# Attention of a hybrid diffusion step: order of the rounds written out, scores of two heads in row halves, final norm on token partitions

## The chip, the cores and the metric

One core of a Trainium2 chip runs the whole program; its other cores are idle. The metric is the time of one execution in microseconds (us), the median of several. Five engines work side by side, each through its own queue in order: TensorE (PE; its weight loads have a row of their own, PEld), VectorE (DVE), ScalarE (ACT), GpSimd (POOL) and SyncE (SP), which here only issues transfers. A transfer that SP issues stands in SP's queue until its buffer is free, and all that is behind it stands too.

## The reference, cut to what matters

```python
x = x_prompt                                    # 128 tokens; then the same for 256 latent tokens
for l in range(2):
    sm, cm, gm, sf, cf, gf = adaln(cond, w_ada[l], b_ada[l])      # silu(cond) @ w_ada + b_ada
    h = rmsnorm(x, norm_mix_g[l]) * (1 + cm) + sm
    if l == 0:                                  # attention, 16 heads of 64
        q, k, v = qkv_proj(h, w_qkv[0])
        mix = merge_heads(attend(q, k, v)) @ w_attn_out[0]
    else:
        mix = chunk_gmlp(h, ...)
    x = x + gm * mix
    h = rmsnorm(x, norm_ffn_g[l]) * (1 + cf) + sf
    x = x + gf * conv_ffn(h, ...)               # width 2816, depthwise conv of width 3
y = rmsnorm(x, norm_final_g)
# attend, context: softmax(q k^T / 8) v over the 128 context keys
# attend, latent (grid of 4 x 64): softmax over [4 x 16 window: q k^T / 8 + rpb | 128 cached keys: q k^T / 8]
```

All data is float32. Outputs are y for both groups and the context keys and values.

## The kernel before, in words

The 384 tokens (128 context, 256 latent) lie on the free axis: `x[k]`, k = 0 to 7, holds 128 features by 384 tokens. Every weight block of 128 x 1024 (a unit of eight 128 x 128 pieces) is loaded by `load` (line 88): SP issues the transfer into a staging tile `st` (pool `stg`, three buffers), ACT rounds it to `hi` (line 96), DVE makes the rest `lo` (line 97). A product is three matmuls, hi x hi, hi x lo, lo x hi (`mac`, lines 103 to 105); PE does 24 of them for one unit.

Attention works on pairs of heads, t = 0 to 7. `keys(t)` makes the 128 features of a pair's keys (24 matmuls), copies them to `kT` (line 439) beside the cached keys, sends the context part out from POOL's queue (`out_skT`, line 440), and builds for each head a tile `ks` with the rounded keys on 64 partitions and their rest on the other 64. `queries(t)` builds `qd` (the rounded queries twice, lines 456 and 457) and `ql`. So a score block of one head (`score`, lines 464 and 465) is a contraction over all 128 partitions, for two latent row blocks (b = 0, 1; 384 keys each) and, with b = 0, the context rows (128 keys). `bias(t)` loads six runs of 64 numbers for each of 64 partitions and each of two rows and two heads (line 473), reversed in DVE's read and added to a mask (line 479). `scores` adds the bias over 256 columns with a running maximum (line 502), takes the maximum of the rest (506, 507, 511), exponentiates on ACT with the sum (486) and normalizes on DVE (487, 488). `turned` transposes a head's probabilities on PE (lines 523 to 528) and copies them to `pT` on ACT (524, 529). `values(t)` multiplies by the values, the two heads in the two column halves of the array (line 538), and splits the result to `ohi`, `olo`. `Ada` computes the modulation of the rest of the layer between the rounds: three blocks of `w_ada` per round, in the array's four column strips (line 190).

The Tile framework's scheduler decides in which order the instructions of a round stand on each engine, from its own model of when data is ready; the loop at the end of `attention` only gives the program order from which it starts. It mixes the splits of later weights, the exponentials and the queries of the next pair freely on ACT, and decides where on SP the loads stand. `kT` and the `ks` tiles have two buffers. The scores of a head use the two banks of `ps_sc` one after another.

After the last pair come the eight output units (`w_o`, from line 560 on, the first three without their last piece until the last pair's values are there), each followed by `residual` (line 366): gate and add on DVE (line 368), the square for the next norm (269, 271), and `early` (336, 337), which prepares the first units of the feed-forward part, for which `norm_first` (line 340) multiplies before the norm is known. The sums of squares are made on PE (line 280) at the place where the program has them.

At the end `rms` makes the inverse norm on token partitions, spreads it over all partitions with three matmuls (line 294), DVE multiplies each `x[k]` with it (line 742), and eight transfers of 192 KB leave from SP's and ACT's queues (line 743).

## Time and profile before

| | us |
|---|---|
| median of 3 runs (1028.15 to 1030.63) | 1030.49 |
| the profiled execution | 1030.51 |
| its span, first to last instruction | 1028.7 |
| outside the span | 1.8 |
| PE busy | 1001.3 (97%) |
| VectorE busy | 796.0 (77%) |
| ScalarE busy | 496.2 (48%) |

The busy shares are means over stages that differ: normalization and values up to 63 us, the rounds of attention and its output units up to 245 us, two feed-forward parts of 280 us each with the gating layer between them, and the final norm. An engine's idle time counts only where it ends last, so a stage is read by its windows, its waits and its timeline. PE's granted clock has a row of its own: 1.00 is 2.4 GHz, 0.50 is 1.2 GHz.

### The profile page before, as it was taken

What the parts mean: (1) busy time and instruction counts of PE and PEld (TensorE: products, weight loads), DVE (VectorE), ACT (ScalarE), POOL (GpSimd) and SP (SyncE); (2) the same over time, 40 slices, a digit from 0 to 9 for tenths busy, and PEclk for the clock granted to TensorE, in tenths of its full rate; (3) what the DMA queues carried; (4) which work ended last, traced back from release to release, by engine and by line L of the source; (5) the groups of instructions that cost most, each with busy time, mean ns of one, the idle gap of its engine ahead of it and who ended that gap; (6) DMA issues with size and microseconds to landing.
All of it is one profiled execution on the core that took longest, in us unless ns stands there. A gap on an engine that the chain in (4) does not pass through costs nothing.

```text
span 1028.7 us, 16012 instructions
## 1 busy us (share of the span) xinstructions
PE 1001.3 (97%) x5964; PEld 953.1 (93%) x5964; DVE 796.0 (77%) x1697; ACT 496.2 (48%) x862; POOL 14.1 (1%) x29
## 2 busy tenths in 40 slices
PE   7999897999999999999999999999999999999996
PEld 5787786899999999999998889999999999999995
DVE  3557777657998888899989989888598777777553
ACT  3357666656754555433345334433385444443330
POOL 1000000000000000000000000000000000000000
PEclk8999898999999999999999999999999999999998
DMA  7867766623355545476637756666325443335521
GB/s 282 308 196 204 204 192 219 217 76 141 108 185 166 165 156 159 135 237 216 217 123 248 245 167 191 183 204 194 106 83 164 143 124 123 124 113 174 163 63 62
DMA packets 64717, 174.32 MB, mean 169 GB/s; under 512 B 18800, under 2 KB 24064, under 8 KB 64640
## 3 DMA queue, kind: packets, MB, share of 16 engines
q1 hardware_dynamic: 63632, 171.46, 52.9%
q8 instruction: 47, 0.77, 0.3%
q0 software_dynamic: 432, 1.06, 0.3%
q10 hardware_dynamic: 576, 0.79, 0.2%
q14 instruction: 30, 0.25, 0.1%
HBM read 170.66 MB, written 2.62 MB: 168 GB/s over the span
## 4 chain that ended last, share of the span: by engine, by line
PE 88%; DMA 4%; DVE 3%; issue 2%; ACT 2%; POOL 0%; SPq 0%; POOLq 0%; DVEq 0%; ACTq 0%
PE bank L103 28%; PE bank L104 27%; PE bank L105 27%; DMA st<-in_w_qk 1%; PE bank L704 1%; PE bank L145 1%; DMA st<-in_w_o 1%; DMA btr<-in_rpb 1%; PE bank L190 1%; PE bank L538 1%; DMA out_skT<-kT 1%; PE bank L280 1%; PE bank L294 0%; ACT hi L96 0%; DMA cond<-in_cond 0%
## 5 line engine op out<-in xcount | busy, mean ns | idle before, releaser
L96 ACT CAST hi<-st 128x1024 fp32r<-128x1024 f32 (+1 forms) x216 | 222.6, 1033 | 325.8 <-PE bank L104 261.6
L104 PE MATMUL bank<-hlo,hi 128*128 128x384 f32 (+1 forms) x960 | 325.7, 339 | 0.0
L105 PE MATMUL bank<-hhi,lo 128*128 128x384 f32 (+1 forms) x960 | 325.6, 339 | 0.0
L103 PE MATMUL bank<-hhi,hi 128*128 128x384 f32 (+1 forms) x960 | 325.1, 339 | 0.0
L97 DVE TENSOR_TENSOR lo<-st,hi 128x1024 fp32r<-128x1024 f32 (+1 forms) x216 | 259.5, 1202 | 84.7 <-ACT hi L96 84.3
L103 PEld LDWEIGHTS bank<-hhi,hi 128*128 128x128 f32 x960 | 181.7, 189 | 0.9 <-issue 0.8
L105 PEld LDWEIGHTS bank<-hhi,lo 128*128 128x128 f32 x960 | 181.7, 189 | 0.0
L104 PEld LDWEIGHTS bank<-hlo,hi 128*128 128x128 f32 x960 | 181.0, 189 | 0.1
L248 DVE CUSTOM_DVE_ANT_0 junk<-adw,cs 128x1024 bf16<-128x1024 f32 x112 | 136.6, 1220 | 1.0
L105 PE MATMUL bank<-ahi,lo 128*128 128x384 f32 x352 | 118.9, 338 | 0.0
L104 PE MATMUL bank<-alo,hi 128*128 128x384 f32 x352 | 118.9, 338 | 0.0
L103 PE MATMUL bank<-ahi,hi 128*128 128x384 f32 x352 | 118.7, 338 | 0.0
L104 PEld LDWEIGHTS bank<-alo,hi 128*128 128x128 f32 x352 | 66.1, 188 | 0.0
L105 PEld LDWEIGHTS bank<-ahi,lo 128*128 128x128 f32 x352 | 66.1, 188 | 0.0
L103 PEld LDWEIGHTS bank<-ahi,hi 128*128 128x128 f32 x352 | 66.1, 188 | 0.0
L103 PE MATMUL bank<-hi,hhi 128*128 128x512 f32 x144 | 57.7, 404 | 1.8 <-ACT hhi L322 1.8
L105 PE MATMUL bank<-hi,hlo 128*128 128x512 f32 x144 | 57.5, 399 | 0.0
L104 PE MATMUL bank<-lo,hhi 128*128 128x512 f32 x144 | 57.4, 398 | 0.0
L368 DVE SCALAR_TENSOR_TENSOR x<-bank,mod,x 128x128 f32<-128x128 f32 x64 | 23.9, 413 | 38.8 <-PE bank L105 38.8
L103 PE MATMUL bank<-mhi,hi 128*128 128x384 f32 x128 | 43.3, 339 | 0.0
L105 PE MATMUL bank<-mhi,lo 128*128 128x384 f32 x128 | 43.2, 337 | 0.0
L104 PE MATMUL bank<-mlo,hi 128*128 128x384 f32 x128 | 43.1, 337 | 0.0
(150 smaller groups left out, 1262.5 us busy)
## 6 DMA issues: line engine op xcount, KB each, us to landing
st<-in_w_up SPq DMA_DIRECT2D x88, 512.0 KB, 3.6
adw<-in_w_adaT SPq DMA_DIRECT2D x56, 512.0 KB, 3.6
adw<-in_w_ada SPq DMA_DIRECT2D x40, 512.0 KB, 6.1
st<-in_w_down SPq DMA_DIRECT2D x32, 512.0 KB, 3.7
st<-in_w_qk SPq DMA_DIRECT2D x16, 512.0 KB, 7.1
st<-in_w_gu SPq DMA_DIRECT2D x16, 512.0 KB, 4.2
st<-in_w_gv SPq DMA_DIRECT2D x16, 512.0 KB, 4.5
st<-in_w_gout SPq DMA_DIRECT2D x16, 512.0 KB, 4.5
```

The lines of the kernel that those rows point to most:

```text
L96: nc.scalar.copy(hi[:, :n], st[:, :n])
L97: nc.vector.tensor_tensor(lo[:, :n], st[:, :n], hi[:, :n].bitcast(F32), ALU.subtract)
L103: nc.tensor.matmul(out, a[0], b[0], start=start, stop=False)
L104: nc.tensor.matmul(out, a[0], b[1], start=False, stop=False)
L105: nc.tensor.matmul(out, a[1], b[0], start=False, stop=stop)
L145: nc.tensor.matmul(pa[32 * j:32 * j + 32, 0:P], cond_s[:, 4 * hf + kk, :], w[hf][:, kk, P * q:P * q + P], start=(kk == 0), stop=(kk == 3), ...
L190: nc.tensor.matmul(self.pa[32 * j:32 * j + 32, 0:256], cond_s[:, k, :], t[:, 256 * j:256 * j + 256], start=(k == 0), stop=(k == KD - 1), t ...
L248: tc.keep_in_program_order(nc.vector.tensor_tensor_reduce(self.junk, t, self.cs[c], 1.0, 0.0, ALU.mult, ALU.add, m[:, c:c + 1]))
L280: mm = nc.tensor.matmul(ss[:, 2 * b:2 * b + 2], src[:, b * P:(b + 1) * P], ones[:, 0:2], start=(i == 0 and b == 0), stop=(i == 1 and b == 2))
L368: nc.vector.scalar_tensor_tensor(x[m][:, a:b], ps[:, a:b], mod(l, gate, m, c), x[m][:, a:b], ALU.mult, ALU.add)
L538: nc.tensor.matmul(pv[64 * hh:64 * hh + 64, cols], vv[:, P * t + 64 * hh:P * t + 64 * hh + 64], pT[hh][:, o:o + n], start=start, stop=stop ...
L704: nc.tensor.matmul(pm[:, b * P:b * P + P], vn[g // 4][:, b, (g % 4) * P:(g % 4) * P + P], ws[:, g % 2, :], start=True, stop=True)
```

## The change: what it does

1. The attention stage from the first weight of the keys to the last piece of output unit 3 stands inside `tc.manual_schedule` for PE, ACT, DVE and SP: on these engines the program's order is the order of issue. POOL keeps its own.
2. Loads are apart from splits: `fetch` issues the next unit's transfer as soon as a staging tile has been split, `ready` splits the unit that came first. The order is keys 0, queries 0, keys 1, queries 1, ..., then the output units.
3. Both heads are scored together (`scores(b, ...)`): one tile of rounded keys and one of their rest (`khi`, `klo`), the same for queries (with the scale's sign turned). A head's contraction is over its own 64 partitions, three matmuls for each block, and the two heads alternate, into two banks. `qd` and `ks` are gone, and with them the zeroed halves.
4. The sign of the scores is turned, so the maximum becomes a minimum over all 384 columns in one DVE instruction with the bias (zeros stand between its parts, since the columns now lie as 128 latent, 128 cached, 128 latent), and `exp` takes scale -1. The reciprocals of a block are one instruction.
5. The bias of a pair comes in two transfers of 64 x 2 runs of 219 numbers (876 bytes); the six overlapping pieces are picked in DVE's read. `kT` and `btr` have one buffer.
6. The tail of attention is written out: where the last pair's transposes, values 6 and 7 and output units 0 to 3 stand.
7. At the end the eight `x[k]` are transposed to token partitions on PE while the norm is computed; three DVE and three ACT instructions multiply with the inverse norm of each token, and six transfers of 256 KB leave. The output `y` is token-major, so the host no longer transposes.

```diff
-    def sums(pin=False):
+    def sums(pin=False, between=None):
         ss = bank(ps_tb)
         for i, src in enumerate((sq["acc"], sq["last"])):
+            if i and between is not None:
+                between()
...
+        KPARTS = ((V[:, 1], 0), (cv, 256), (V[:, 2], 512))
+        def weights():
+            for t in range(NPAIR):
+                yield w_qk[1, t]
+                yield w_qk[0, t]
+            yield from (w_o[m] for m in range(KD))
+        coming = weights()
+        staged, units = [], []
+        def fetch():
+            src = next(coming, None)
+            if src is None:
+                return
+            st = stg.tile([P, 1024], F32, name="st", tag="st")
+            nc.sync.dma_start(st.rearrange("p (a b) -> p a b", b=P), src)
+            staged.append(st)
+        def ready():
+            st = staged.pop(0)
+            hi = whp.tile([P, 1024], F32R, name="hi", tag="hi")
+            lo = wlp.tile([P, 1024], F32R, name="lo", tag="lo")
+            split(hi, lo, st)
+            fetch()
+            units.append(tuple(p.rearrange("p (a b) -> p a b", b=P) for p in (hi, lo)))
...
+        def cache(t):
+            kT = wkp.tile([P, 512], F32, name="kT", tag="kT", bufs=1)
+            nc.sync.dma_start(kT[:, 256:384], ckT_in[:, t, :])
+            return kT
+        def keys(t, kT, p):
+            nc.scalar.copy(kT[:, 0:256], p[:, 0:256])
+            nc.scalar.copy(kT[:, 384:512], p[:, 256:384])
             nc.gpsimd.dma_start(skT_out[:, t, :], kT[:, 0:NPR])
-            ks = [wkp.tile([P, 512], F32R, name="ks", tag=f"ks{hh}", bufs=2) for hh in range(2)]
+            k = [wkp.tile([P, 512], F32R, name=n, tag=n) for n in ("khi", "klo")]
+            split(*k, kT)
+            return k
+        def queries(p):
+            q = [wkp.tile([P, NT], F32R, name=n, tag=n) for n in ("qhi", "qlo")]
+            s = -HD ** -0.5
+            nc.scalar.activation(q[0], p[:, :NT], AF.Copy, scale=s)
+            nc.vector.scalar_tensor_tensor(q[1], p[:, :NT], s, q[0].bitcast(F32), ALU.mult, ALU.subtract)
+            return q
...
+        def scores(b, q, k, sc):
+            for cols, qs, ks in ((slice(0, NT), NPR + b * P, slice(NPR, 512)),
+                                 (slice(NT, 512), 0, slice(0, NPR)))[:2 - b]:
+                for i, (qp, kp) in enumerate(((0, 0), (0, 1), (1, 0))):
+                    for hh in range(2):
+                        nc.tensor.matmul(sc[hh][:, cols], q[qp][HS[hh], qs:qs + P], k[kp][HS[hh], ks],
+                                         start=i == 0, stop=i == 2)
...
+        def exps(b, sc, pr, pc):
+                nc.vector.tensor_tensor_reduce(
+                    sc[hh][:, :NT], sc[hh][:, :NT],
+                    bt[:, hh, 2 - 2 * b:5 - 2 * b].rearrange("p g c -> p (g c)"),
+                    1.0, 3e38, ALU.add, ALU.min, st[:, 0, hh:hh + 1])
...
+        order = tc.manual_schedule(engines={mybir.EngineType.PE, mybir.EngineType.Activation,
+                                            mybir.EngineType.DVE, mybir.EngineType.SP})
+        order.__enter__()
+        for _ in range(3):
+            fetch()
+        kT, btr = cache(0), bias_load(0)
+        nc.sync.dma_start(cv, cv_in)
+        ada.load(3)
+        ready()
+        p = products()
+        ready()
+        K = keys(0, kT, p)
+        p = products()
+        ready()
+        bias(btr)
+        Q = queries(p)
         old = None
-        pT = None
         for t in range(NPAIR):
-            new = [scores(t, 0, qT, kT, bt)]
+            last = t == NPAIR - 1
+            pr = [wkp.tile([P, 2, NT], F32, name="pr", tag="pr", bufs=4) for _ in range(2)]
+            pc = [wkp.tile([P, NPR], F32, name="pc", tag="pc", bufs=4) for _ in range(2)]
+            sc = [bank(ps_sc) for _ in range(2)]
+            scores(0, Q, K, sc)
+            if not last:
+                kT, btr = cache(t + 1), bias_load(t + 1)
+            e = exps(0, sc, pr, pc)
             if old is not None:
-                pT = [turned(0, old)]
-            if t < NPAIR - 1:
-                kT2 = keys(t + 1)
-                bt2 = bias(t + 1)
+                two = turn(*old[0])
+            normalized(*e)
             if old is not None:
-                pT.append(turned(1, old))
-            new.append(scores(t, 1, qT, kT, bt))
-            if t < NPAIR - 1:
-                qT, kT, bt = queries(t + 1), kT2, bt2
+                pT = [turned(0, two)]
+            if not last:
+                p = products()
+            ready()
+            sc = [bank(ps_mm if last else ps_sc) for _ in range(2)]
+            scores(1, Q, K, sc)
+            if last:
+                ada.run(3)
+            else:
+                K = keys(t + 1, kT, p)
+            e = exps(1, sc, pr, pc)
             if old is not None:
-                values(t - 1, pT)
-            old = new
-            ada.load(3)
-            ada.run(3)
+                pT.append(turned(1, turn(*old[1])))
+            normalized(*e)
+            if not last:
+                p = products()
+                ready()
+                bias(btr)
+                Q = queries(p)
+                if old is not None:
+                    values(t - 1, pT)
+                ada.run(3)
+                ada.load(3)
+                old = [(pr[hh], pc[hh]) for hh in range(2)]
...
+        output(0, range(6), ps_mm)
+        ready()
+        values(6, pT, ps_sc)
+        output(1, range(6), ps_sc)
+        ready()
+        pT = [turned(0, turn(pr[0], pc[0]))]
+        output(0, (6,))
+        output(1, (6,))
+        pT.append(turned(1, turn(pr[1], pc[1])))
+        output(2, range(7), ps_mm)
+        ready()
+        values(7, pT)
+        output(3, range(7), ps_sc)
         ada.flush()
-        head = []
-        for m in range(KD):
-            w = load(w_o[m])
-            po = bank(ps_mm if m != 2 else ps_sc)
-            n = KD - 1 if m < 3 else KD
-            for k in range(n):
-                mac(po[:, :NT], wsel(w, k, allm), (ohi[k], olo[k]), k == 0, k == KD - 1)
-            if m < 3:
-                head.append((w, po))
-            else:
-                residual(0, GM, m, po, (0, SF, CF))
-            if m == 0:
-                pT = [turned(0, old)]
+        for m in range(4):
+            output(m, (7,))
+            residual(0, GM, m, out[m][1], (0, SF, CF))
+            if m == 1:
+                ready()
+        order.__exit__(None, None, None)
...
-    R = rms()
-    for k in range(KD):
-        nc.vector.tensor_tensor(x[k], x[k], R[:, :NT], ALU.mult)
-        (nc.sync, nc.scalar)[k % 2].dma_start(yT_out[:, k, :], x[k])
+    with tc.tile_pool(name="fin", bufs=1) as pool:
+        turned = [[bank(q) for q in two] for two in ((ps_ta, ps_ad), (ps_sc, ps_sc), (ps_mm, ps_mm))]
+        def turn(ks):
+            for k in ks:
+                for b in range(3):
+                    o = (k % 4) * P
+                    tc.keep_in_program_order(nc.tensor.transpose(
+                        turned[b][k // 4][:, o:o + P], x[k][:, b * P:(b + 1) * P], ident))
+        r = inverse(sums(True, lambda: turn(range(3))))
+        turn(range(3, KD))
+        for b in range(3):
+            for half in range(2):
+                y = pool.tile([P, 512], F32, name=f"y{b}{half}")
+                if half:
+                    nc.scalar.activation(y, turned[b][half], AF.Copy, scale=r[:, b:b + 1])
+                else:
+                    nc.vector.tensor_scalar(y, turned[b][half], r[:, b:b + 1], None, ALU.mult)
+                (nc.sync, nc.scalar)[half].dma_start(y_out[b, :, 512 * half:512 * half + 512], y)
```

On ACT, in round t = 5, from the last exponentials of the pair to its predecessor's outputs (`pr`, `pc` probabilities, `hi` a unit's rounded half, `qd` or `qhi` the next pair's queries). Before:

```order
L96 CAST hi_2263<-st_2262 128x1024
L486 ACTIVATE pr_1852,st_1854<-bank_1855,st_1854 128x384
L96 CAST hi_2303<-st_2302 128x1024
L486 ACTIVATE pc_1853,st_1854<-bank_1855,st_1854 128x128
L486 ACTIVATE pr_1852,st_1854<-bank_1870,st_1854 128x384
L456 ACTIVATE qd_1910<-bank_1885 64x384
L457 ACTIVATE qd_1910<-bank_1885 64x384
L96 CAST hi_2354<-st_2353 128x1024
```

Now:

```order
L534 ACTIVATE pr_1700,st_1795<-bank_1780,st_1795 128x384
L534 ACTIVATE pr_1701,st_1795<-bank_1781,st_1795 128x384
L556 COPY pT_1809<-bank_1800 128x512
L557 COPY pT_1809<-bank_1801 128x384
L108 CAST hi_1840<-st_1597 128x1024
L482 ACTIVATE qhi_1848<-bank_1815 128x384
L108 CAST ohi4_181<-bank_1852 128x384
```

Three splits of output units stood among the exponentials and ahead of the queries; now one split stands there, behind the exponentials and the transposed copies, of a unit that was fetched three splits earlier.

On DVE, in the same half of the round (`lo` a unit's rest, `bt` the bias, `qlo` the queries' rest, `olo` the outputs' rest). Now:

```order
L541 TENSOR_SCALAR pr_1700<-pr_1700,st_1795 128x384
L541 TENSOR_SCALAR pr_1701<-pr_1701,st_1795 128x384
L109 TENSOR_TENSOR lo_1841<-st_1597,hi_1840 128x1024
L507 TENSOR_TENSOR bt_718<-mask_161,btr_1720 128x3x128 x2
L483 SCALAR_TENSOR_TENSOR qlo_1849<-bank_1815,qhi_1848 128x384
L109 TENSOR_TENSOR olo4_189<-bank_1852,ohi4_181 128x384
```

The queries' rest, on which PE's next score block waits, is the last but one of a chain that begins with the exponentials.

On SP, from the load of pair 6's cached keys to that of pair 7's. Before:

```order
L434 DMA kT_1792<-in_ckT 128x128
L93 DMA st_1794<-in_w_qk 128x1024
L473 DMA btr_1833<-in_rpb 64x6x64 x2
L176 DMA adw_1737<-in_w_ada 128x1024
L176 DMA adw_1739<-in_w_ada 128x1024
L473 DMA btr_1833<-in_rpb 64x6x64 x2
L93 DMA st_1879<-in_w_qk 128x1024
L176 DMA adw_1929<-in_w_ada 128x1024
L93 DMA st_1995<-in_w_qk 128x1024
L434 DMA kT_1993<-in_ckT 128x128
```

Now:

```order
L468 DMA kT_1718<-in_ckT 128x128
L497 DMA btr_1720<-in_rpb 64x2x219 x2
L448 DMA st_1778<-in_w_o 128x1024
L448 DMA st_1844<-in_w_o 128x1024
L176 DMA adw_1882<-in_w_ada 128x1024
L176 DMA adw_1884<-in_w_ada 128x1024
L176 DMA adw_1886<-in_w_ada 128x1024
L468 DMA kT_1906<-in_ckT 128x128
```

The keys and the bias are now asked for first in a round, the bias in two transfers for four, and the two units that follow are already output units, three splits ahead.

## Rows read from the trace of the kernel before

**Rows 1.** The page: the granted clock in 40 slices of 25.7 us, and the chain of work that ended last, as shares of the span by engine.

```profile
PEclk8999898999999999999999999999999999999998
...
PE 88%; DMA 4%; DVE 3%; issue 2%; ACT 2%; POOL 0%; SPq 0%; POOLq 0%; DVEq 0%; ACTq 0%
```

**Rows 2.** The windows of three stages (rounds of attention and their outputs, first feed-forward part, final norm): length, busy time and count of each engine, granted clock, share of the DMA engines, GB/s.

```profile
56.00:250.00 194.00, 183.93 (x1210) 161.47 (x1210) 131.29 (x385) 123.56 (x273) 5.79 (x10) 0.96 0.60 186
...
250.00:530.00 280.00, 280.00 (x1603) 279.82 (x1602) 251.47 (x513) 135.70 (x215) 0.85 (x1) 1.00 0.55 171
...
1016.00:1028.70 12.70, 2.68 (x15) 2.24 (x14) 4.90 (x14) 1.14 (x2) 0.85 (x1) 0.61 0.35 124
```

**Rows 3.** What PE waited for between 63 and 250 us: total, times, longest.

```profile
PE bank L464 <- ACT qd L457: 6.9, 4, 4.7
PE bank L464 <- ACT pc L486: 1.8, 1, 1.8
PE bank L206 <- ACT ada_sb L195: 0.8, 1, 0.8
```

**Rows 4.** The windows of the two stretches at the lower clock in the rounds (columns as in rows 2).

```profile
121.10:127.92 6.82, 6.07 (x25) 4.86 (x26) 5.27 (x19) 4.32 (x11) 0.00 (x0) 0.50 0.80 236
172.30:179.12 6.82, 4.69 (x23) 2.98 (x27) 6.64 (x17) 4.99 (x13) 0.00 (x0) 0.50 0.59 215
```

**Rows 5.** The timeline around the longest gap, 168 to 176 us: start, length, engine, line, and in brackets the idle time before it and its releaser.

```profile
170.01 1.04 ACT L96 CAST hi<-st 128x1024 fp32r<-128x1024 f32 x1 [4.95 <-DMA st<-in_w_o]
...
173.86 0.48 ACT L457 ACTIVATE qd<-bank 64x384 fp32r<-64x384 f32 x1
...
174.40 1.01 PE L464 MATMUL bank<-ks,qd 128*128 128x384 f32 x2 [4.66 <-ACT qd L457]
```

**Rows 6.** The timeline of PE in a round without a wait, 135 to 147 us: end of a product, values, modulation, first score block, transposes, second score block.

```profile
135.36 0.34 PE L105 MATMUL bank<-hhi,lo 128*128 128x384 f32 x1
...
135.89 0.34 PE L105 MATMUL bank<-hhi,lo 128*128 128x384 f32 x1
136.16 1.08 PE L538 MATMUL bank<-pT,V 128*64 128x256 f32 x8
...
137.83 1.50 PE L190 MATMUL bank<-adw,cond_s 128*32 128x256 f32 x24
139.26 0.45 PE L464 MATMUL bank<-ks,qd 128*128 128x384 f32 x1
...
139.72 0.22 PE L464 MATMUL bank<-ks,qd 128*128 128x128 f32 x1
139.78 0.27 PE L465 MATMUL bank<-ks,ql 128*128 128x128 f32 x1
139.89 0.39 PE L464 MATMUL bank<-ks,qd 128*128 128x384 f32 x1
...
140.30 0.60 PE L523 MATMUL bank<-ident,pr 128*128 128x128 f32 x4
...
145.95 0.42 PE L464 MATMUL bank<-ks,qd 128*128 128x384 f32 x1
...
146.95 0.34 PE L103 MATMUL bank<-hhi,hi 128*128 128x384 f32 x1
```

**Rows 7.** Groups of instructions, shapes kept apart: count, busy us, mean ns of one, idle before.

```profile
L97 DVE TENSOR_TENSOR lo<-st,hi 128x1024 fp32r<-128x1024 f32 x200 | 244.3, 1222 | 82.5 <-ACT hi L96 82.2
L96 ACT CAST hi<-st 128x1024 fp32r<-128x1024 f32 x200 | 209.2, 1048 | 294.9 <-PE bank L104 241.0 <-PE bank L105 20.4 <-issue 11.4
...
L486 ACT ACTIVATE pr<-bank,st 128x384 f32<-128x384 f32 x32 | 18.4, 578 | 9.8 <-DVE st L507 9.6
...
L502 DVE CUSTOM_DVE_ANT_0 bank<-bank,bt 128x256 f32<-128x256 f32 x32 | 13.3, 440 | 1.1 <-PE bank L465 0.7
...
L445 DVE TENSOR_TENSOR ks<-kT,ks 64x512 fp32r<-64x512 f32 x16 | 11.0, 686 | 5.5 <-ACT ks L444 5.1
...
L524 ACT COPY pT<-bank 128x512 f32<-128x512 f32 x16 | 9.4, 586 | 9.9 <-PE bank L523 9.8
...
L479 DVE TENSOR_TENSOR bt<-btr,mask 128x768 f32<-128x768 f32 x8 | 7.7, 958 | 4.3 <-issue 2.6 <-DMA btr<-in_rpb 1.7
```

**Rows 8.** What SP's queue waited for between 60 and 215 us, and transfers between 73 and 197 us: KB each, median us from issue to landing.

```profile
SPq L434 <- DMA out_skT<-kT: 39.4, 5, 9.9
...
btr<-in_rpb SPq DMA_DIRECT2D x24, 96.0 KB, 7.1
...
out_skT<-kT POOLq DMA_DIRECT2D x7, 64.0 KB, 6.0
```

**Rows 9.** The timeline of DVE at the end of attention: the first and the last of the output units' residual adds.

```profile
217.53 1.39 DVE L368 SCALAR_TENSOR_TENSOR x<-bank,mod,x 128x128 f32<-128x128 f32 x4 [3.34 <-PE bank L105]
...
239.65 0.74 DVE L368 SCALAR_TENSOR_TENSOR x<-bank,mod,x 128x128 f32<-128x128 f32 x2 [0.95 <-PE bank L105]
```

**Rows 10.** The timeline of the final norm.

```profile
1015.50 0.73 PE L280 MATMUL bank<-ones,sqacc 128*128 128x2 f32 x6
...
1017.05 0.83 PE L280 MATMUL bank<-ones,t 128*128 128x2 f32 x6 [0.83 <-ACT t L269]
...
1021.47 3.81 DVE L742 TENSOR_TENSOR x<-x,bank 128x384 f32<-128x384 f32 x8 [1.81 <-PE bank L294]
1022.05 3.12 SPq L743 DMA_DIRECT2D out_yT<-x  x4
```

More of the change, by code (lines that the diff above doesn't have):

```diff
@@ L171, in load @@
             for _ in range(n):
[L172 removed]
+                if len(self.ready) == ADA_BUFS or not self.todo:
                     return
@@ L462, in score @@
-        def score(out, hh, q, ks, qs, cs):
-            qd, ql = q
-            nc.tensor.matmul(out, qd[hh][:, qs], ks[hh][:, cs], start=True, stop=False)
-            nc.tensor.matmul(out, ql[hh][:, qs], ks[hh][:, cs], start=False, stop=True)
-        def bias(t):
-            btr = wkp.tile([P, 2, 6, 64], F32, name="btr", tag="btr", bufs=1)
-            for rr in range(2):
-                for hh in range(2):
-                    nc.sync.dma_start(
-                        btr[64 * rr:64 * rr + 64, hh],
-                        bass.AP(rpb_in.tensor,
-                                rpb_in.offset + (2 * t + hh) * 465 + (5 - rr) * 31 - 48,
-                                [[1, 64], [31, 6], [1, 64]]))
-            bt = wkp.tile([P, 2, 6, 64], F32, name="bt", tag="bt", bufs=2)
-            nc.vector.tensor_tensor(bt.rearrange("p h s c -> p (h s) c"),
-                                    btr.rearrange("p h s c -> p (h s) c")[:, :, ::-1],
-                                    mask.unsqueeze(1).to_broadcast([P, 12, 64]), ALU.add)
-            return bt
@@ new lines, in normalized, with turn @@
+        def normalized(st, ps):
+            nc.vector.reciprocal(st[:, 2, :len(ps)], st[:, 1, :len(ps)])
+            for i, p in enumerate(ps):
+                nc.vector.tensor_scalar(p, p, st[:, 2, i:i + 1], None, ALU.mult)
+        def turn(pr, pc):
+            ta, tb = bank(ps_ta), bank(ps_tb)
+            for g in range(3):
+                for b in range(2):
+                    o = g * 256 + b * P
+                    nc.tensor.transpose((ta[:, o:o + P] if g < 2 else tb[:, o - 512:o - 512 + P]),
+                                        pr[:, b, g * P:g * P + P], ident)
+            nc.tensor.transpose(tb[:, 256:384], pc, ident)
+            return ta, tb
@@ L537, in part, with turned, values @@
+        def turned(hh, two):
+            pT = wkp.tile([P, 896], F32, name="pT", tag=f"pT{hh}", bufs=1)
+            nc.scalar.copy(pT[:, 0:512], two[0])
+            nc.scalar.copy(pT[:, 512:896], two[1][:, :384])
+            return pT
+        def values(t, pT, pool=ps_mm):
+            pv = bank(pool)
             def part(hh, cols, vv, o, n, start, stop):
@@ L546, in values @@
             split(ohi[t], olo[t], pv[:, :NT])
-        kT, qT, bt = keys(0), queries(0), bias(0)
+        order = tc.manual_schedule(engines={mybir.EngineType.PE, mybir.EngineType.Activation,
[8 more added lines that the diff above has]
+        p = products()
@@ new lines, in attention, with output @@
+        out = {}
+        def output(m, ks, pool=None):
+            if m not in out:
+                out[m] = (units.pop(0), bank(pool))
+            for k in ks:
+                mac(out[m][1][:, :NT], wsel(out[m][0], k, allm), (ohi[k], olo[k]), k == 0, k == KD - 1)
+        output(0, range(6), ps_mm)
[6 more added lines that the diff above has]
+        output(1, (6,))
@@ new lines, in attention @@
+        pT.append(turned(1, turn(pr[1], pc[1])))
[3 more added lines that the diff above has]
+        output(3, range(7), ps_sc)
+        ada.flush()
+        for m in range(4):
+            output(m, (7,))
+            residual(0, GM, m, out[m][1], (0, SF, CF))
+            if m == 1:
+                ready()
+        order.__exit__(None, None, None)
+        for m in range(4, KD):
+            output(m, range(KD), ps_mm if m % 2 else ps_sc)
+            if m < KD - 2:
+                ready()
+            residual(0, GM, m, out[m][1], (0, SF, CF))
```

132 lines of the change are left out of this document (44 added, 88 removed).

## The prediction

> **What bounds the kernel now.** I read the page first. The chain that ended last is TensorE for 88% of the span, and the granted clock is full in most slices, with dips in the fifth and the seventh [rows 1]. The windows show where: the first feed-forward part has nothing to give (280 us of PE in 280 us), while the rounds of attention, 56 to 250 us, have PE busy for 183.9 of 194 us at a mean clock of 0.96, and the final norm takes 12.7 us with PE nearly idle [rows 2]. So the change can win at two places: 10.1 us of idle PE in the rounds, and what the clock loses there.
>
> The waits of PE say what the idle time is: 6.9 us behind the queries' copies on ACT, 1.8 us behind an exponential, 0.8 us behind the modulation's copy [rows 3]. The longest gap shows how it comes about. At 170.0 us ACT, whose queue is in order, starts a split for which it had waited 4.95 us, because a weight of the output units had not landed; exponentials and query copies stood behind it, and PE's scores began 4.66 us late [rows 5]. VectorE and ScalarE are not full in the rounds, so their order costs, not their work. The clock fell to 0.50 (1.2 GHz) in two stretches of 6.82 us, each after such gaps; PE was busy in them for 6.07 and 4.69 us, half of which, 5.4 us, the full clock would have saved [rows 4]. The stock in the rounds is thus 10.1 + 5.4 = 15.5 us.
>
> **The change, part by part.** The sum is made against the profiled execution (1030.51 us, of which the span is 1028.7), which equals the median of the runs.
>
> *Loads apart from splits: -15.5 us of stalls.* A unit's transfer now starts three splits, a round and a half or some 22 us, before its split. The bias of a pair no longer sends 256-byte runs: its transfers took 7.1 us each, and the keys' loads on SP stood 39.4 us in all behind outgoing keys, with everything queued behind them [rows 8]. No split should wait for data, so I take the whole stock away and add back what the written order makes PE wait for.
>
> *New waits: +6.5 us (2.5 to 14).* I walk through one round with the durations of rows 7, from the end of the first score block. DVE adds the bias over 384 columns; 256 take 0.44 us and a 384-column add from PSUM 0.48 a step [rows 7, 10], so I take 0.65 with its read-out, twice: 1.3. ACT's exponentials, 0.58 each and less for the context, end at 2.6, the two transposed copies (0.59 and 0.5) at 3.7, the split of the queries' weight at 4.7; DVE's `lo` (1.22) ends at 5.9. PE meanwhile makes transposes (0.7), the keys product (24 matmuls at 0.176, 4.2 us) and the second score block, and wants that weight at 6.8: in time. Keys copies and `khi` end at 6.5, `klo` (0.69) at 7.1, the next biases at 8.4, exponentials 9.1, copies 10.2 (PE wants them for the values at 11.0), the next split 11.3, `qhi` 11.8, `lo` 12.5, the bias 13.6 (0.96 in one before, 1.1 in two), `qlo` 14.1. PE ends values (1.67) and modulation (1.43) at 14.2 [rows 6], starts the scores with `qhi` and wants `qlo` some 0.4 us later. So the round is PE's, with half a microsecond to spare in the chain over ACT and DVE: I allow 1.5 us for rounds 1 to 6 together.
>
> At the start 0.5 us may be lost because two splits now stand ahead of the last normalized values; round 0 has nothing between the queries' product and its scores (one copy, 0.5 us, and part of `qlo`) and its next weight comes 0.3 us late: 1.1. In the last round nothing covers ACT: the second transposes wait 0.5 us for the copies of the first, and values 6 wait 1.4 us for the second copies: 1.9. After it, DVE had 22.1 us from the first residual add to the last [rows 9], with little idle; now it starts one product later (3.7 us) against the same end, so the sums of squares may come 1.5 us late. Together 6.5. The low end is half of the walk's certain part; the high end adds 1 us to each of seven rounds.
>
> *Scores in row halves: -0.6 us (-3.4 to +6.4).* Before, a pair's two blocks take 1.04 and 1.00 us [rows 6], 16.3 us for eight pairs. No row shows two matmuls side by side in row halves, so I bound it. A step of 384 columns is 0.176 us, one of 128 columns 0.06 (or 0.11 where its weight load shows) [rows 6]. If two heads cost as much as one, a round has 6 x 0.176 + 3 x 0.06 = 1.23 us; if they go one after another, 2.46. Between lies a case where the array overlaps but its 18 weight loads do not: six two-column matmuls end 0.83 us after the first starts, so one load takes about 0.11 [rows 10], and 18 make 1.93. The change of the array's division costs too: the first values start 0.27 us after the product's last matmul began, where the step is 0.176 [rows 6], so 0.09 each, four a round, 0.38. The three cases are 1.6, 2.3 and 2.85 us a round: -3.4, +2.2 and +6.4 us. The values, in column halves, cost eight pairs of passes in 1.67 us, one pair at a time [rows 6], so I expect overlap and take the middle of the first two, -0.6. The Trainium skill ("TensorEngine Tiling (Array Packing)", Key Properties) warns that a change of tiling mode drains the array; the 0.09 us above is this trace's size of it.
>
> *Less work on DVE and ACT: 0.* Some 2.9 us of DVE and 2 us of ACT go from each round; PE's product and values cover them. If that cover went, they would be what the chain's half microsecond consists of.
>
> *Final norm: -1.3 us (-0.5 to -2.0).* Before, three matmuls spread the norm over the partitions, DVE has waited 1.81 us for them when its eight multiplications start at 1021.47 (3.81 us), and the first transfer leaves at 1022.05 [rows 10]. Now the norm is used where it is made: DVE and ACT start some 1.6 us earlier, at about 1019.9, after 0.2 us lost to nine transposes ahead of the last sums, and the first 256 KB leave at 1020.6. The bytes are the same and keep all queues busy for some 4.3 us, so the end moves by the first start, less 0.2.
>
> Sum: -15.5 + 6.5 - 0.6 - 1.3 = -10.9 us, so **1019.6 us**.
>
> **The rivals.**
>
> *The row halves run fully side by side and the order fits.* For it: PE has cover in every round of the walk. Against: half a microsecond is little. -15.5 + 3 - 3.4 - 1.3 = -17.2: 1013.3 us. The Trainium skill ("TensorE: Matmul & The Clock Gate", Part 3) says that weight loads overlap running matmuls when the row groups differ; by that rule this is the case to expect, and no run here shows it yet.
>
> *No overlap in row halves.* +6.4 in place of -0.6: 1026.6 us. For it: no row shows the form.
>
> *The gain moves into new waits.* The written order is fixed, and ACT's lateness passes on to DVE and PE as before. At 2 us in each of six rounds, beside the 5 us counted elsewhere, new waits are 17 us, and 1030.1 us remain.
>
> *Slower: the keys' chain.* `kT` has one buffer now; its load stands on SP behind the outgoing keys of the pair before (6.0 us from issue to landing, waits up to 9.9 us [rows 8]) and ahead of the units. In the walk the outgoing keys are issued at 5.9 us of the round and have landed by 12.5, SP asks at 14.2, and the keys must be there 5.8 us into the next round. If landing takes over 13 us, `khi` is late, and with it the second biases, exponentials, copies and `qlo`; each round then stands for 3 us or more, and the clock falls as in rows 4. Seven rounds at 3 us and four falls at 2.7 are 32 us: 1030.5 - 10.9 + 32 = 1051 us. It decides from 1.6 us a round on.
>
> **How the numbers follow.** My case has 0.52, the full overlap 0.2, no overlap 0.08, the gain moved 0.1, the keys' chain 0.1. The time is that of my case. Its own terms run from -15.5 + 2.5 - 3.4 - 2 = -18.4 to -15.5 + 14 + 2.2 - 0.5 = +0.2; I cut the tails and range from 1010 to 1028 us, which holds the first two cases, most of the third, and leaves out some 0.2. A measurement of this kernel can tell 0.3%, 3.1 us, from no change: faster 0.8 (the first two and half of the third), same 0.1, slower 0.1.
>
> **What would show it.** Right: PE's waits in the rounds fall from 10 to about 6 us, and the clock is 1.00 from 25 us on; no split waits for a transfer; two score matmuls of different heads start within a few hundredths of a microsecond; a round takes 15 to 15.5 us; the first `y` transfer leaves 1.4 us earlier, counted from the last product. Wrong: PE waiting in each round for `qlo` or `khi` (the chain is longer than in the walk); score blocks over 1.5 us (no overlap); a lower clock again; or a stall of several microseconds where the first feed-forward part begins.

## The result, and the profile after

The changed kernel takes **1021.46 us** (median of 4 runs, 1018.24 to 1022.09), before 1029.46 us beside it: ratio 0.9916, 95% interval 0.989 to 0.9942. That is 8.0 us less; 1019.6 us (10.9 less) had been forecast, with a range of 1010 to 1028. The profiled execution took 1021.36 us, of which the span is 1019.6; it is the one compared below with the profiled one of before.

Where the time went, by the starts of the same matmuls on TensorE in both traces:

| stretch | before, us | after, us | change | forecast |
|---|---|---|---|---|
| start of the span to the first product of attention | 63.47 | 63.81 | +0.3 | +0.5 |
| to the first values (start and round 0) | 36.05 | 33.98 | -2.1 | |
| five rounds, values to values | 90.64 | 80.76 | -9.9 | |
| last of these values to the last sums | 825.34 | 829.29 | +4.0 | +3.4 |
| last sums to the end | 13.20 | 11.76 | -1.4 | -1.3 |
| sum | 1028.7 | 1019.6 | -9.1 | -10.9 |

(To the second and third lines together belonged -13.5 us of the forecast: the stock of -15.5, the row halves' -0.6, and 1.1 and 1.5 of new waits; they gave -12.0. The +3.4 is the last round and the boundary to the feed-forward part.)

The page, clock and chain; these answer to [rows 1]:

```profile
PEclk8999999999999999999999999999999999999999
PE 91%; DMA 3%; ACT 2%; DVE 1%; issue 1%; SPq 1%; POOL 0%; POOLq 0%; ACTq 0%
```

The dips of the clock in the fifth and the seventh slice are gone. The windows of the rounds, of a new stretch at the lower clock and of the final norm (columns as in [rows 2]):

```profile
56.00:250.00 194.00, 187.65 (x1303) 163.62 (x1303) 120.00 (x302) 109.94 (x258) 6.64 (x10) 0.99 0.54 183
213.64:217.05 3.41, 3.41 (x12) 3.41 (x12) 2.74 (x7) 3.41 (x7) 0.00 (x0) 0.50 0.00 0
1007.84:1019.60 11.76, 4.08 (x37) 3.82 (x36) 3.46 (x9) 3.09 (x5) 0.85 (x1) 0.84 0.36 134
```

PE is busy for 187.65 us in place of 183.93, and the low clock has shrunk from two stretches of 6.82 us [rows 4] to one of 3.41. It lies right behind an idle gap of 1.86 us and costs some 1.6 us: a step of 384 columns takes 0.32 us in it, in place of 0.176. What PE waits for between 56 and 250 us (answers to [rows 3]; total, times, longest):

```profile
PE bank L190 <- DMA adw<-in_w_ada: 2.0, 3, 0.8
PE bank L103 <- DVE x L374: 1.9, 1, 1.9
PE bank L206 <- ACT ada_sb L195: 1.0, 2, 0.5
PE bank L517 <- ACT qhi L482: 0.6, 1, 0.6
PE bank L517 <- DVE qlo L483: 0.6, 2, 0.3
PE bank L105 <- DVE lo L109: 0.2, 1, 0.2
```

They add up to 6.3 us, about what was forecast (6), but in other places: modulation weights that land late (last round) and a result bank that waits for a residual add (213 us). The rounds did not become 15 to 15.5 us: they are 16.3, 16.8, 15.3, 15.9 and 16.4 us. SP's queue and ACT's show why (start, length, engine, line; idle time before in brackets):

```profile
85.11 2.36 SPq L176 DMA_DIRECT2D adw<-in_w_ada  x3
87.57 0.38 SPq L468 DMA_DIRECT2D kT<-in_ckT  x1
```
```profile
94.83 0.62 ACT L108 CAST khi<-kT 128x512 fp32r<-128x512 f32 x1 [2.19 <-DMA kT<-in_ckT]
```

The cached keys (64 KB) are issued right behind three modulation weights of 512 KB. They land after 7.6 us (median), where before they took 2.0; ACT waits for them in six rounds, 9.6 us in all, and with it the exponentials and copies; so a split did wait for a transfer, one of the prediction's signs that failed. The values, 1.66 us where nothing holds them, then take 2.38, 2.36, 1.66, 1.92 and 1.90 us from the first start to the next product.

The row halves do run side by side. PE's timeline in a round (answers to [rows 6]):

```profile
118.99 0.44 PE L517 MATMUL bank<-khi,qhi 64*128 64x384 f32 x2
119.27 0.34 PE L517 MATMUL bank<-klo,qhi 64*128 64x384 f32 x2
119.45 0.34 PE L517 MATMUL bank<-khi,qlo 64*128 64x384 f32 x2
119.63 0.23 PE L517 MATMUL bank<-khi,qhi 64*128 64x128 f32 x2
119.69 0.28 PE L517 MATMUL bank<-klo,qhi 64*128 64x128 f32 x2
119.80 0.28 PE L517 MATMUL bank<-khi,qlo 64*128 64x128 f32 x2
120.00 0.88 PE L549 MATMUL bank<-ident,pr 128*128 128x128 f32 x6
120.75 0.42 PE L103 MATMUL bank<-hhi,hi 128*128 128x384 f32 x1
```

Each row holds both heads' matmuls, which start within 0.01 us; the block takes 1.01 us, the other one 0.72, together 0.3 less than before. One after another, the first block's six steps of 0.176 us and six of 0.06 would take 1.4 us. But a product of 24 matmuls beside the blocks now takes 4.38 us in place of 4.30, and seven transposes 0.74 in place of 0.69. The final norm (answers to [rows 10]):

```profile
1007.84 0.73 PE L282 MATMUL bank<-ones,sqacc 128*128 128x2 f32 x6
1009.45 0.78 PE L282 MATMUL bank<-ones,t 128*128 128x2 f32 x6
1012.11 2.07 DVE L836 TENSOR_SCALAR y<-bank,rr 128x512 f32<-128x512 f32 x3
1012.82 0.92 ACTq L837 DMA_DIRECT2D out_y<-y  x2
```

The first transfer leaves 4.98 us after the first sums; before it was 6.55.

### The profile page after: what moved, and what is told of

Same layout as the page of the kernel before. It is cut to its first block, busy times and chain, and to the rows that moved or that the text cites. A ratio compares the mean times of both kernels' runs of the same rounds, so it can differ in the third digit from the quotient of the medians.

```text
span 1019.6 us, 15979 instructions
## 1 busy us (share of the span) xinstructions
PE 998.2 (98%) x6030; PEld 948.6 (93%) x6030; DVE 775.7 (76%) x1588; ACT 480.6 (47%) x841; POOL 14.7 (1%) x29
## 4 chain that ended last, share of the span: by engine, by line
PE 91%; DMA 3%; ACT 2%; DVE 1%; issue 1%; SPq 1%; POOL 0%; POOLq 0%; ACTq 0%
PE bank L103 28%; PE bank L105 28%; PE bank L104 28%; DMA kT<-in_ckT 2%; DMA adw<-in_w_ada 1%; PE bank L781 1%; PE bank L145 1%; PE bank L566 1%; PE bank L517 1%; PE bank L190 1%; PE bank L549 1%; PE bank L282 0%; ACT pr L534 0%; SPq L66 0%; PE bank L300 0%
## 5 line engine op out<-in xcount | busy, mean ns | idle before, releaser
L96 ACT CAST hi<-st 128x1024 fp32r<-128x1024 f32 (+1 forms) x192 | 197.7, 1031 | 302.3 <-PE bank L104 249.0
L97 DVE TENSOR_TENSOR lo<-st,hi 128x1024 fp32r<-128x1024 f32 (+1 forms) x192 | 229.9, 1198 | 67.9 <-ACT hi L96 67.6
```

Source lines behind the costliest of these rows:

```text
L96: nc.scalar.copy(hi[:, :n], st[:, :n])
L97: nc.vector.tensor_tensor(lo[:, :n], st[:, :n], hi[:, :n].bitcast(F32), ALU.subtract)
```

## The experiments

Each run is compared with the kernel before on its own chip, so the ratios are what can be set beside 0.9916; 0.001 is 1.03 us.

| kernel | median, us | ratio to before, 95% | against the changed kernel, by ratio |
|---|---|---|---|
| e1 old final norm | 1022.89 | 0.9917 (0.9894 to 0.9941) | 0 us |
| e2 heads apart | 1021.58 | 0.9896 (0.9871 to 0.9921) | -2 |
| e3 scheduler's order | 1014.74 | 0.9839 (0.9823 to 0.9856) | **-8** |
| e4 stacked scores | 1037.14 | 1.006 (1.0039 to 1.008) | **+15** |
| e6 keys' load early | 1019.68 | 0.9872 (0.985 to 0.9894) | -4.5 |
| e7 output banks | 1021.37 | 0.9894 (0.9873 to 0.9914) | -2 |
| e8 last round | 1018.79 | 0.9872 (0.9852 to 0.9893) | -4.5 |
| e9 three edits | 1015.23 | 0.9837 (0.9815 to 0.9859) | **-8** |
| f1 e3 with stacked scores | 1014.96 | 0.9848 (0.9822 to 0.9874) | -7 |
| f2 e3 with 256-byte bias | 1027.16 | 0.9972 (0.9956 to 0.9989) | +6 |
| f3 e3 with loads at splits | 1018.2 | 0.988 (0.9855 to 0.9905) | -4 |
| f4 four edits | 1015.87 | 0.9862 (0.9832 to 0.9892) | -5.5 |

Differences under some 3 us are within the intervals; for those the traces decide.

**Is the order, or are the parts, the gain? (e3, f1, f2, f3)**

```
-        order = tc.manual_schedule(engines={mybir.EngineType.PE, mybir.EngineType.Activation,
-                                            mybir.EngineType.DVE, mybir.EngineType.SP})
-        order.__enter__()
...
-        order.__exit__(None, None, None)
```

> The changed kernel without the written order: the same instructions, but the scheduler orders them on each engine. If the order is what removed the stalls, waits on TensorE in the rounds come back to about 10 us and a low clock with them: 1027 to 1031 us. If it was the earlier transfers, the larger bias pieces and the lighter score form, the waits stay near 6 us: 1020 to 1023 us.

The opposite of the first: without the written order the kernel is 8 us faster. What PE waits for between 56 and 250 us in it, all of it:

```profile
PE bank L517 <- ACT pc L534: 0.8, 1, 0.8
PE bank L190 <- DMA adw<-in_w_ada: 0.7, 1, 0.7
```

Its rounds take 15.06 us (99.67 to 114.73), 15.96 where a piece of the modulation ends, and the clock stays at full from 23 us to the tail. So the written order costs what the prediction called new waits, and the gain is in the other parts. From this kernel one part at a time was put back. The scheduler then orders each kernel anew, so such a difference holds the part and the order that came with it:

```
-                nc.sync.dma_start(
-                    btr[64 * rr:64 * rr + 64],
...
-                            [[1, 64], [465, 2], [1, 219]]))
+                for hh in range(2):
+                    nc.sync.dma_start(
+                        btr[64 * rr:64 * rr + 64, hh],
...
+                                [[1, 64], [31, 6], [1, 64]]))
...
```

> The kernel without the written order, with the bias loaded in pieces of 256 bytes as before (four transfers a pair in place of two). If the small pieces held up the queue and the transfers behind them, the keys' loads land later, ScalarE waits for them, and the time rises by 3 us or more: 1018 us and up. If they were never on the path, 1014 to 1016 us.

This part is the large one: 13.7 us by the ratios, with the order that the scheduler makes for it. The transfers between 73 and 197 us, in f2 and then in e3 (packets; KB, median us to landing):

```profile
DMA packets 18095, 24.39 MB, mean 197 GB/s; under 512 B 12052, under 2 KB 12948, under 8 KB 18085
...
st<-in_w_qk SPq DMA_DIRECT2D x10, 512.0 KB, 9.1
...
out_skT<-kT POOLq DMA_DIRECT2D x7, 64.0 KB, 4.9
```
```profile
DMA packets 9307, 25.07 MB, mean 202 GB/s; under 512 B 1120, under 2 KB 3680, under 8 KB 9296
...
st<-in_w_qk SPq DMA_DIRECT2D x10, 512.0 KB, 4.2
...
out_skT<-kT POOLq DMA_DIRECT2D x7, 64.0 KB, 1.9
```

The bytes are about the same. The medians are not of like with like, since the scheduler now puts the modulation's weights ahead of the attention's; the first 512 KB behind a pair's bias are: they land after 7.8 to 12.2 us in f2 (median 8.3) and 3.9 to 4.6 in e3 (4.2), for seven pairs each. The kernel before shows it without a change of order: between 76 and 153 us, weights of `w_qk` issued right behind a pair's last bias transfer landed after 7.9 to 10.6 us (five, median 10.0), those issued right behind the cached keys after 3.6 to 7.9 (six, median 4.0). The weight of the longest gap [rows 5] had been issued at 159.9 us, behind four bias transfers and three modulation weights, and landed after 9.9.

How it reaches PE can be followed once in f2. The outgoing keys issued at 98.2 us stand among bias pieces and take 7.7 us, and all on SP stands behind them (51.8 us in f2 in all, but 51.6 in e3 too):

```profile
106.18 0.33 SPq L468 DMA_DIRECT2D kT<-in_ckT  x1
106.74 2.61 SPq L498 DMA_DIRECT2D btr<-in_rpb  x3
...
112.28 1.57 SPq L448 DMA_DIRECT2D st<-in_w_qk  x2
```

ACT waits 9.9 us for that weight, to 121.4, and PE for the copies behind it:

```profile
ACT hi L108 <- DMA st<-in_w_qk: 18.5, 5, 9.9
```
```profile
PE bank L568 <- ACT pT L558: 5.4, 1, 5.4
```

ACT's wait is 5.4 us in all in e3. So f2 loses 3.8 us against e3 up to the first values and 7.7 in this one round; the clock is at 0.50 for 6.83 us twice, from 87.4 and 121.6 us on. Two later rounds take 15.07 and 15.35 us with the same pieces in them. The longest gap of before does not come back, neither here nor in f3. Next, the loads at their splits:

```
         def ready():
+            fetch()
             st = staged.pop(0)
...
             split(hi, lo, st)
-            fetch()
...
-        for _ in range(3):
-            fetch()
```

> The kernel without the written order, with each weight of the attention loaded where it is split, as before, in place of three splits ahead. If the early transfers took the stalls away, as the prediction has it, ScalarE waits for weights again, by up to 5 us at a time, and the time rises to 1020 to 1030 us. Rival: three staging buffers and a queue that runs ahead already bring the transfers early, and the waits of before had another cause: 1014 to 1017 us.

Between the two: 4 us by the ratios. ACT waits 8.7 us for weights, and PE 3.0 us at one place, with a low clock behind it; after round 0 the staging buffers bring the transfers early enough (first values 2.9 us later than in e3, then the same rounds). Last, the scores as before:

```
-            split(*k, kT)
+            for hh in range(2):
+                a, b = HS[hh], HS[1 - hh]
+                nc.scalar.copy(k[hh][a], kT[a])
+                nc.vector.tensor_tensor(k[hh][b], kT[a], k[hh][a].bitcast(F32), ALU.subtract)
...
+                nc.scalar.activation(q[hh][a], p[a, :NT], AF.Copy, scale=s)
+                nc.scalar.activation(q[hh][b], p[a, :NT], AF.Copy, scale=s)
+                nc.vector.scalar_tensor_tensor(qlz[hh][a], p[a, :NT], s, q[hh][a].bitcast(F32),
+                                               ALU.mult, ALU.subtract)
...
+                        nc.tensor.matmul(sc[hh][:, cols], (q[hh], qlz[hh])[i][:, qs:qs + P],
+                                         k[hh][:, ks], start=i == 0, stop=i == 1)
```

> The kernel without the written order (1014.7 us), with the scores as before: keys stacked on 128 partitions, queries doubled, two matmuls per head. In the written order this form cost 15 us. If the copies that the row halves save on ScalarE and VectorE are what removed the stalls of before, whatever the order, waits on TensorE come back here too: 1022 to 1030 us. If the cost lay in the written order alone, and a scheduler places the extra copies where there is room, 1015 to 1018 us.

No difference that can be told; in the trace five rounds take 78.2 us in place of 77.1, and the first values come 1.1 us earlier. But in the written order:

> The changed kernel with the scores as before: both parts of the keys stacked on 128 partitions, queries doubled, two matmuls per head in place of three in row halves; all else, the order too, as changed. An undisturbed round has the same length on TensorE in both kernels (15.10 us before, 15.07 us after), so the form gives TensorE nothing. My theory now: its worth lies on ScalarE and VectorE, where the stacked form costs 2.0 and 1.2 us more in each round, in a chain that already makes TensorE wait; then each of seven rounds grows by 1.5 to 2.5 us: 1031 to 1038 us. The prediction's own step (less work on DVE and ACT: 0, since TensorE's products cover it) gives 1021 to 1023 us.

15 us. Of 15.5 us of PE's waits there, 12.4 are for those copies, or (`L206`) for one that stands behind them in ACT's queue:

```profile
PE bank L206 <- ACT ada_sb L195: 5.6, 2, 3.0
PE bank L528 <- ACT qd L488: 4.5, 7, 1.1
PE bank L528 <- DVE qlz L489: 2.3, 8, 1.0
```

The rounds take 16.6 us, those in which a piece of the modulation ends 18.2 and 21.3. But not all of it is the length of the copies. The edit writes copy, copy, rest for one head and then for the other, and ACT stands between the heads until DVE has made the first head's rest:

```profile
ACT qd L487 <- DVE qlz L489: 13.3, 8, 1.8
```

In f1 this wait is 3.1 us (5 times). So the same work off the critical engine is free in one order and costs 15 us in another; what the copies alone cost in the written order, with all four ahead of the two rests, was not run.

**Do the halves overlap because of the alternation? (e2)**

```
-                for i, (qp, kp) in enumerate(((0, 0), (0, 1), (1, 0))):
-                    for hh in range(2):
+                for hh in range(2):
+                    for i, (qp, kp) in enumerate(((0, 0), (0, 1), (1, 0))):
```

> The same 18 score matmuls a round, but the three of one head first and then the three of the other, so that neighbours on TensorE mostly share a row half. If the two halves do run side by side in the changed kernel, the blocks grow from 1.02 and 0.72 us to about 1.6 and 1.15 us (serial steps of 0.176 and 0.06 us): 1.0 us a round, 8 us in eight rounds, less what the waits of the rounds take up: 1025 to 1029.5 us. If the equal start times in the records say nothing and the array works one matmul after another anyway, the blocks stay as they are: 1021.5 us.

The time is the same, but for neither reason given. PE's timeline, in a round like the one above:

```profile
167.70 0.45 PE L517 MATMUL bank<-khi,qhi 64*128 64x384 f32 x2
167.98 0.34 PE L517 MATMUL bank<-klo,qhi 64*128 64x384 f32 x2
168.15 0.34 PE L517 MATMUL bank<-khi,qlo 64*128 64x384 f32 x2
```

Three matmuls of head 0 stand ahead of the first of head 1 in the queue, yet head 1's first starts 0.01 us behind head 0's first: each half works down its own chain. The blocks are 1.01 and 0.73 us again.

**The final norm by itself (e1)**

```
-        r = inverse(sums(True, lambda: turn(range(3))))
...
+    R = rms()
+    for k in range(KD):
+        nc.vector.tensor_tensor(x[k], x[k], R[:, :NT], ALU.mult)
+        (nc.sync, nc.scalar)[k % 2].dma_start(y_out[:, k, :], x[k])
```

> The changed kernel with the final norm of before (norm spread by three matmuls, eight multiplications, output feature by feature); attention as changed. If the new final norm gives what the trace shows (last sums to end 13.2 us before, 11.8 us after), the time rises by 1.4 us, to 1022.9 us, and the stretch from the first matmul of the last sums to the end of the span is 13.2 us again. Rival: the end is bound by the bytes that leave and by their landing alone; then nothing changes, 1021.5 us.

The time can't tell (1.4 us within intervals of 2.4). The trace can: from the first matmul of the last sums, at 1009.88, to the end of the span, 1023.0, it is 13.1 us again.

**The three waits of the written order (e6, e7, e8, e9)**

```
+        kT = cache(1)
...
-                kT, btr = cache(t + 1), bias_load(t + 1)
+                btr = bias_load(t + 1)
...
                 K = keys(t + 1, kT, p)
+                if t < NPAIR - 2:
+                    kT = cache(t + 2)
```

> The changed kernel, in its written order, with one load moved: the cached keys of the pair after next are fetched as soon as the old keys are split, in place of behind the next modulation weights. In the changed kernel ScalarE waits 9.6 us, six times, for that load, whose landing takes 7.0 to 7.7 us behind three 512 KB loads. If those waits are the first link of what TensorE loses in rounds 1 to 6 (about 1.9 us at the values and 1.5 us at the queries' low part), they go and the time falls by about 3 us, to 1018.5 us. Rival: ScalarE's wait is slack, and the values wait for the copies for another reason: 1021.5 us, TensorE's rounds as long as before.

The link holds: the keys land in 1.8 to 2.8 us, ACT no longer waits for them, the rounds take 15.07 us (98.07 to 113.14), those with the end of a modulation piece 16.1, and the values of round 6 start at 175.54 in place of 178.55. Then the 3 us are given back:

```profile
184.00 1.08 PE L190 MATMUL bank<-adw,cond_s 128*32 128x256 f32 x8 [1.94 <-DMA adw<-in_w_ada]
```

The modulation's weights of the last round come no earlier than before, PE idles longer for them, and the clock is at 0.50 for 6.8 us from 183.7 on. The last sums start at 1007.85 us, where the changed kernel has them at 1007.84. The ratio says 4.5 us less, and its interval touches that of the changed kernel. The profiled execution is the longest of six (1021.37 us at a granted clock of 0.988; the others 1016.45 to 1019.99 at 0.990 to 0.995), so the loss in the last round need not be that large in the others: not settled.

```
-            output(m, range(KD), ps_mm if m % 2 else ps_sc)
+            output(m, range(KD), ps_sc if m % 2 else ps_mm)
```

> The changed kernel with the result banks of output units 4 to 7 exchanged: unit 4 takes a bank that is free since the values, in place of one that waits for the second residual add. The wait of 1.9 us at 213 us and the stretch at the lower clock behind it (3.41 us, 1.7 us lost) should go: 1018 us. Rival: VectorE is the bound behind the outputs, as the prediction's 1.5 us said; then the wait comes back at the sums of squares before the first feed-forward part, and the time stays at 1021.5 us.

Mostly the rival. Wait and low clock go, and the last 108 output matmuls take 20.24 us in place of 22.69; but from there to the last sums it takes 777.85 in place of 775.93 us, since the splits of the next weights are late:

```profile
PE bank L103 <- ACT hi L96: 0.8, 1, 0.8
PE bank L105 <- DVE lo L97: 0.3, 1, 0.3
```

```
+            if last:
+                ready()
             e = exps(0, sc, pr, pc)
...
             if last:
-                ada.run(3)
+                output(0, range(6), ps_mm)
...
         ready()
+        ada.run(3)
         values(6, pT, ps_sc)
```

> The changed kernel with another order in its last round alone: the weight of the first output unit is split before that round's exponentials, its products follow the last scores at once, and the modulation's three steps come after them, when their weights have landed. TensorE waits 2.5 us for those weights in the changed kernel. My theory: they go, the first output products start about 2.5 us earlier, and the time falls by 2 to 2.5 us, to 1019 us. Rival: the copies of the turned probabilities set the pace there (the prediction's 1.9 us for the last round); then the values of pair 6 start as late as before: 1021.5 us.

As expected: PE has no wait for the modulation left, and the values of pair 6 start at 189.14 us in place of 192.34, against the rival. The first output products start at 183.58 in place of 189.00, mostly because the modulation's steps now follow them. The last sums come at 1005.28 in place of 1007.84; 0.7 us of that was there before the last round, which gives 1.9.

> The three edits together (keys' load earlier, banks exchanged, last round reordered). If the three waits are separate they add up to about 9 us: 1012.5 us, somewhat under the 1014.7 us of the kernel without a written order. If one stands behind another (VectorE at the end of attention above all), 1015 to 1018 us.

1015.23 us: by the ratio as fast as the scheduler's order. Somewhat less than the three singly promised, since e7's gain is partly lost at the boundary: from the last values to the last sums it takes 803.1 us, in the changed kernel 804.2, in e3 800.6. A fourth edit spread the modulation's steps:

```
             scores(0, Q, K, sc)
+            if old is not None:
+                ada.run(1)
...
-                ada.run(3)
+                ada.run(2 if t else 1)
...
```

> The written order with the three edits (1015.2 us), and the modulation's steps shared out: one behind the first scores of a round, two at its end, so that the end of a piece falls between rounds and TensorE does not wait for its copy (two waits of 0.5 us go). Each extra change between scores and modulation may cost about 0.1 us, seven times. Expected: 1014.5 us, within the noise of the kernel with three edits; slower by 1 us or more would say that the copies of the scores are now late.

Nothing gained: the wait at `L206` is gone and one of 0.7 us for `qlo` has come.

## Why the prediction was right, point by point

- **Direction and time**: right, 1021.46 in 1010 to 1028; 8.0 us gained of 10.9. That it came so near is in part luck: the stock was some 4 us too small and the new waits 5.7, and the two errors mostly cancel.
- **The stock, -15.5**: right in kind, too small. Put back in the scheduler's order, the bias pieces are worth 13.7 us and the early loads 4, together 17.9; they are not strictly a sum, since e3 gains 16.6 us in all, final norm included. The step named the early transfers first; the larger pieces, with the order that came with them, carry three quarters. The five rounds of before held 90.64 - 5 x 15.1 = 15.1 us above the stall-free length (some 0.8 of it the modulation's transposes), and the start and round 0 gave 2.1 more. A part of what the forecast missed is that idle time counts from a matmul's modelled end, 0.34 us after its start, where the next could have started after 0.176: each stall hides some 0.16 us.
- **New waits, +6.5**: right as a price of the written order: without it 8 us go, and three edits give the same. Size and places were wrong: rounds 1 to 6 lost 4.4 us, not 1.5; the last round 2.5 for modulation weights, not 1.9 for copies; the boundary 2.0 (by the starts) at a bank and 1.6 of clock, not 1.5 for sums of squares; start and round 0 0.3 and 1.4 (0.5 and 1.1). Up to the last sums the change is -7.7 us, where the steps gave -9.6. With these 12.2 us and 0.2 for the row halves the stock must have been 19.7: 14.3 in the rounds, 3.5 in round 0, and some 2 in the last stretch, where the trace of before shows no wait; these stay open.
- **Row halves, -0.6**: full overlap, as that rival said, and as the Trainium skill has it ("TensorEngine Tiling (Array Packing)", Key Properties: tiles load and multiply independently); e2 agrees, 0.01 us between the halves' starts. Yet not its -3.4: a stall-free round is 15.07 us against 15.10, 0.2 us in eight rounds. The full overlap allowed 0.38 us a round for changes of the array's division; measured are 0.5 over the bare steps in the blocks (1.73 against 1.23), weight loads included, and 0.26 more in the products and transposes beside them.
- **Less work on DVE and ACT, 0**: right in the scheduler's order (f1), not in the written one, where putting it back costs 15 us (e4), a part of them through the wait between ACT and DVE that came with the edit. There product and values did not cover it, as the prediction feared in its next sentence.
- **Final norm, -1.3**: 1.4 by the trace; e1's 13.1 us agree; its time alone does not show it.
- **The keys' chain**: the mechanism of the slower rival was there, late keys and late `khi`, at 0.2 to 0.7 us at the values of four rounds instead of 3, and behind the modulation's weights, not the outgoing keys (2.2 us after, 6.0 before).

Open: the larger bias pieces alone in the kernel before, and the small ones in the written order or in a fixed order, were not run. So the delay of the transfers behind them is shown, but not how much of the 13.7 us is the size of the pieces, how much the number of transfers and how much the scheduler's new order.

## What to carry to other kernels

Before costing a new order of work, take the transfers apart by packet size: a small strided load can cost little itself and still delay everything queued behind it. A written order is worth its slack on each queue, DMA queues included: give the small load that the next step needs its place ahead of the large ones, and try the scheduler's order beside it. Judge saved work on an idle engine together with the order, and with the hand-overs between engines that come with it, not by itself.

## What was not expected of the hardware

- The two row halves of the array do not share one order: with three matmuls of one head queued ahead, the other head's first started 0.01 us after the first (e2). So that each engine works through its queue in order holds for PE within a row half, not between the two.
- With bias pieces of 256 bytes in place of 876, in four transfers a pair in place of two, the first 512 KB behind them landed after 7.8 to 12.2 us in place of 3.9 to 4.6 (f2, e3). The Trainium skill ("DMA: Bandwidth & Descriptors", Specifications) puts the least transfer for line rate at 512 bytes; the runs agree in direction.
- A gap of 1.86 us was followed by 3.41 us at 1.2 GHz (from 213.64 us on); in e6 gaps of 1.94 and 0.21 us went with 6.8 us of it.
